# The durations of matmuls that a list scheduler assumes, set to their measured spacing

## The chip, the core and the metric

The kernel runs on one core of a Trainium2 chip. The core has TensorE (PE: matrix products, accumulated in PSUM), VectorE (DVE), ScalarE (ACT), GpSimd (POOL) and SyncE (SP, which here starts loads), each with its own queue of instructions that it takes in order. The metric is the device time of one launch in microseconds (us), the median of several runs.

## What is computed

A forward pass over 512 tokens of width 1024 through three blocks, in float32. The first (layer A) has four gated linear-attention heads of width 192, the second (layer B) twelve banded attention heads of width 64; both add four heads over 256 memory tokens and are followed by a feed-forward part with a short convolution. The third (block 2) has four differential heads, eight heads with a forget gate, and a feed-forward part. Its attention, cut to what matters here:

```python
dq, dk, dv, fq, fk, fv, fg = jnp.split(rmsnorm_2(x, norm1_g) @ w_in, SPLITS, axis=-1)
log_f = jax.nn.log_sigmoid((fg + b_f).astype(f32))
cum = jnp.cumsum(log_f, axis=1)
# four differential heads: two softmaxes, their difference times the values, then a norm
p = softmax(mask(q1 @ k1.T * scale)) - lam * softmax(mask(q2 @ k2.T * scale))
od = rmsnorm_2(p @ dv, subln_g) * (1.0 - lam_init)
# eight gated heads: the scores get the difference of the summed gates
pf = softmax(causal(fq @ fk.T * scale + cum_q - cum_k))
of = pf @ fv
x = x + concat(od, of) @ w_out
x = x + (silu(h2 @ w_gate) * (h2 @ w_up)) @ w_down
```

## The kernel before

Every float32 product is made of three matmuls: each operand is split into a rounded high piece and a low remainder, and high times high, high times low and low times high are summed in one PSUM tile (`mm3`, L420 to L422; in token-major form L440 to L442). Weights come in pieces of 1024 columns by SP into `wr` (2 buffers); `round` (L380) makes the high piece `wh`, on ScalarE or VectorE, and `sub` (L368) the remainder `wl`, on VectorE or GpSimd. Activations `xs` are held as such pairs, feature-major, so that one projection tile `bd` is 8 weight pieces by 3 matmuls of 512 columns.

An attention head goes: keys and queries are split (`kq`; L1126 and L1130 bring the gated heads' keys and queries out of PSUM, L548 and L549 are DMAs on GpSimd's queue that put the pieces in place); scores on TensorE (L556, L558, L559 into `bs`); mask, maximum, exponential and sum (L571, L574, L575, or L568 for the memory heads); a scaling by the reciprocal (L375 on VectorE or GpSimd, or ScalarE); four transposes on TensorE (L586 into `bt`); the split of the probabilities into `pt` (L592 and L593); the product with the values (L605, L606, or L1084 to L1086 for differential heads, into `bo`). A differential head ends with a norm: L1089 clips, a column sum on TensorE (L479), L1094 to L1098 on VectorE, a broadcast of the 512 factors on TensorE (L490), and L1100. In front of the gated heads stands a chain of its own: transposes of the gates (L1103), a copy, a running sum and its split (L1105 to L1116), and for each head the rows that go into the scores (L1135 into `cb`).

The order of every engine's instructions is not the program's. The program is traced once, a list scheduler (class `Order`) walks it with assumed durations (`duration`, L103) and latencies (`LAT`), and the program is traced again with the order found as order-only edges; all waits stay those of the data. At each step a free engine takes the first instruction, in program order, whose operands are ready by the assumed times and whose tiles are to be had: 3 PSUM banks for `bd`, 2 for scores, 2 for `bt`, 1 for `bo`, and so on. So a projection matmul of a later head fills TensorE while an earlier head's softmax is under way, and how many fill it before the softmax is taken to be ready depends on the assumed duration of a matmul against those of the other engines. `other` (L272) gives an idle engine a rounding, remainder or scaling that would wait longer in another's queue; which engine such an instruction runs on is thus set by the same numbers.

## Time and profile before

| | us |
|---|---|
| runs (3): median, lowest, highest | 1939.57, 1938.87, 1941.28 |
| the profiled execution: span | 1938.4 |
| TensorE busy (8628 instructions) | 1861.8, 96% |
| VectorE busy | 1183.9, 61% |
| ScalarE busy | 868.6, 45% |
| GpSimd busy | 323.8, 17% |

The median of the runs is 1.2 us above the span of the profiled execution. The page gives each engine's busy time, a picture of the span in 40 slices, the queues, the chain that ended last and the costliest lines. On TensorE the end of a matmul is modelled, and one in a row shows as 0.39 us where the next starts 0.23 us after it; the spacing of starts is what counts there. By stage: layer A's attention and projections lie in 25 to 290 us, layer B's in 660 to 866, block 2's in 1275 to 1512; the feed-forward parts are 292 to 660, 866 to 1275 and 1512 to 1922.

### The profile page before, as it was taken

How to read it: one execution, taken by the hardware profiler on the slowest of the kernel's cores; microseconds unless marked ns; L12 is line 12 of the kernel's file. 1: busy time of each engine (PE TensorE's matmuls, PEld its weight loads, DVE VectorE, ACT ScalarE, POOL GpSimd, SP SyncE). 2: the span in 40 equal slices, each digit the busy share in tenths (PEclk: the TensorE clock that was granted, in tenths of full speed). 3: DMA queues.
4: the chain of work that ended last, by engine and by line, in shares of the span. 5: the costliest groups of instructions: out<-in, count | busy, mean ns of one | idle time of the engine just before them, and what ended most of it. 6: DMA issues, size and time to landing. Idle time of an engine off the chain costs nothing.

```text
span 1938.4 us, 23991 instructions
## 1 busy us (share of the span) xinstructions
PE 1861.8 (96%) x8628; PEld 1528.4 (79%) x8628; DVE 1183.9 (61%) x2233; ACT 868.6 (45%) x1651; POOL 323.8 (17%) x335
## 2 busy tenths in 40 slices
PE   7999899999999999889999999989998999999997
PEld 7887688888888878768888888878776788888885
DVE  6969776544555667696654455576989754434433
ACT  5567654432444555574442344344657533323332
POOL 2212111100111202131110011141433111001110
PEclk9999899999999999999999999999999999999998
DMA  4223232222223423223222322333321322232222
GB/s 183 92 99 98 82 98 98 98 86 99 98 91 112 160 92 112 87 86 127 88 98 90 106 96 87 97 115 110 93 82 39 120 88 98 93 102 94 94 92 81
DMA packets 59095, 191.93 MB, mean 99 GB/s; under 512 B 7776, under 2 KB 14304, under 8 KB 57184
## 3 DMA queue, kind: packets, MB, share of 16 engines
q1 hardware_dynamic: 54432, 177.81, 27.4%
q0 software_dynamic: 4544, 12.59, 2.5%
q8 instruction: 68, 1.11, 0.2%
q14 instruction: 51, 0.42, 0.1%
HBM read 174.64 MB, written 6.29 MB: 93 GB/s over the span
## 4 chain that ended last, share of the span: by engine, by line
PE 78%; DVE 10%; ACT 2%; issue 1%; DMA 0%; POOL 0%; DVEq 0%; ACTq 0%; POOLq 0%
PE bd L420 23%; PE bd L421 23%; PE bd L422 23%; DVE ae L571 1%; DVE pt L593 1%; DVE ae L375 1%; PE bt L586 1%; PE bd L441 1%; PE bd L440 1%; PE bd L442 1%; DVE wl L368 1%; PE bs L556 1%; DVE kq L368 1%; ACT ae L574 1%; PE bo L605 1%
## 5 line engine op out<-in xcount | busy, mean ns | idle before, releaser
L380 ACT CAST wh<-wr 128x512 fp32r<-128x512 f32 (+2 forms) x574 | 341.6, 596 | 797.1 <-PE bd L421 676.4
L420 PE MATMUL bd<-xs,wh 128*128 128x512 f32 (+1 forms) x1680 | 656.0, 391 | 9.1 <-ACT wh L380 8.0
L422 PE MATMUL bd<-xs,wl 128*128 128x512 f32 (+1 forms) x1680 | 655.3, 390 | 0.0
L421 PE MATMUL bd<-xs,wh 128*128 128x512 f32 (+1 forms) x1680 | 655.0, 390 | 0.0
L368 DVE TENSOR_TENSOR wl<-wr,wh 128x512 fp32r<-128x512 f32 (+2 forms) x590 | 397.8, 676 | 341.7 <-ACT wh L380 332.0
L420 PEld LDWEIGHTS bd<-xs,wh 128*128 128x128 f32 x1680 | 316.7, 189 | 74.4 <-ACT wh L380 8.0
L421 PEld LDWEIGHTS bd<-xs,wh 128*128 128x128 f32 x1680 | 317.0, 189 | 63.7 <-issue 1.9
L422 PEld LDWEIGHTS bd<-xs,wl 128*128 128x128 f32 x1680 | 316.9, 189 | 63.6 <-issue 1.2
L732 POOL TENSOR_TENSOR te<-te,R 128x512 f32<-128x512 f32 x66 | 85.8, 1300 | 830.6 <-ACT te L731 830.6
L422 PE MATMUL bd<-kq,wl 128*128 128x512 f32 x528 | 208.0, 394 | 0.0
L420 PE MATMUL bd<-kq,wh 128*128 128x512 f32 x528 | 208.0, 394 | 0.0
L421 PE MATMUL bd<-pt,wh 128*128 128x512 f32 x528 | 208.0, 394 | 0.0
L422 PEld LDWEIGHTS bd<-kq,wl 128*128 128x128 f32 x528 | 98.7, 187 | 24.5
L421 PEld LDWEIGHTS bd<-pt,wh 128*128 128x128 f32 x528 | 98.7, 187 | 24.4
L420 PEld LDWEIGHTS bd<-kq,wh 128*128 128x128 f32 x528 | 98.7, 187 | 24.4
L735 DVE TENSOR_TENSOR te<-bd,te 128x512 f32<-128x512 f32 x66 | 45.6, 691 | 104.5 <-PE bd L422 98.6
L720 DVE TENSOR_TENSOR te<-bd,R 128x512 f32<-128x512 f32 x66 | 45.6, 691 | 94.5 <-PE bd L422 94.5
L502 POOL TENSOR_TENSOR ae<-ae,ae 128x512 f32<-128x512 f32 x40 | 58.2, 1455 | 246.8 <-ACT ae L498 211.5
L368 POOL TENSOR_TENSOR wl<-wr,wh 128x512 fp32r<-128x512 f32 (+2 forms) x42 | 56.8, 1353 | 177.1 <-ACT wh L380 119.9
L380 ACT CAST kq<-te 128x512 fp32r<-128x512 f32 (+1 forms) x109 | 67.6, 620 | 38.2 <-DVE te L735 32.0
L586 PE MATMUL bt<-ident,ae 128*128 128x128 f32 x304 | 56.4, 286 | 22.8 <-DVE ae L375 9.7
L440 PE MATMUL bd<-wh,xs 128*128 128x384 f32 (+3 forms) x200 | 65.7, 334 | 6.0 <-ACT wh L380 3.0
(260 smaller groups left out, 2237.1 us busy)
## 6 DMA issues: line engine op xcount, KB each, us to landing
wr<-in_w_g SPq DMA_DIRECT2D x66, 512.0 KB, 3.3
wr<-in_w_u SPq DMA_DIRECT2D x66, 512.0 KB, 3.2
wr<-in_w_d SPq DMA_DIRECT2D x48, 512.0 KB, 3.4
wr<-in_w_d SPq DMA_DIRECT2D x48, 192.0 KB, 2.3
kq<-kq POOLq DMA_DIRECT2D x64, 128.0 KB, 3.1
wr<-in_w_qk SPq DMA_DIRECT2D x12, 512.0 KB, 3.2
v<-in_xT SPq DMA_DIRECT2D x4, 1024.0 KB, 8.7
wr<-in_w_o SPq DMA_DIRECT2D x8, 512.0 KB, 3.3
```

The lines of the kernel that those rows point to most:

```text
L368: self.either("DVE", ("DVE", "Pool"), lambda e: e.tensor_tensor(out=out, in0=a, in1=b, op=ALU.subtract))
L375: return e.tensor_scalar(out=out, in0=a, scalar1=s, scalar2=1.0, op0=ALU.mult, op1=ALU.mult)
L380: self.either("Activation", ("DVE", "Activation"), lambda e: (e.copy if e is self.nc.scalar else e.tensor_copy)(out, a))
L420: mm(o, lhsT=wh, rhs=xh, start=start, stop=False)
L421: mm(o, lhsT=wh, rhs=xl, start=False, stop=False)
L422: mm(o, lhsT=wl, rhs=xh, start=False, stop=stop)
L440: mm(pss[b][:, :ncol], lhsT=x[k][0][:, tb], rhs=hi, start=st, stop=False)
L502: (nc.gpsimd if k < 6 else nc.vector).tensor_tensor(out=sq, in0=acc, in1=sq, op=ALU.add)
L586: self.nc.tensor.transpose(o[:, k * 128:(k + 1) * 128], p[:, k * 128:(k + 1) * 128], self.ident)
L720: nc.vector.tensor_tensor(out=g, in0=pg, in1=R, op=ALU.mult)
L732: nc.gpsimd.tensor_tensor(out=s, in0=s, in1=R, op=ALU.mult)
L735: nc.vector.tensor_tensor(out=h, in0=pu, in1=s, op=ALU.mult)
```

## The change

In `duration`, the two numbers for a matmul on TensorE become larger: for float32 pieces (n columns) from n x 0.4167 + 2.6 ns, at least 107, to n x 0.4167 + 13.3, at least 109; for a plain float32 matmul at least 224 instead of 214. The rest of the diff takes comments and docstrings away.

```diff
         if e == "PE":
             if rd[0][7] == F32R:
-                return max(n * 0.4167 + 2.6, 107)
-            return 109 if getattr(ins, "is_transpose", False) else max(4 * n * 0.4167, 214)
+                return max(n * 0.4167 + 13.3, 109)
+            return 109 if getattr(ins, "is_transpose", False) else max(4 * n * 0.4167, 224)
```

The multiset of TensorE's instructions stays. The orders agree in the feed-forward parts and differ in the attention stretches and the start; about 180 roundings, remainders and scalings of those that may run on several engines change engine.

In the rows below, a name with a number is one tile, before the arrow what is written, behind it what is read. On TensorE, at the end of block 2's fourth differential head: `bt_12366` is its column sum, `bt_12382` the gate transposes, `bd_12891` and `bd_12940` are projections of gated heads (keys and queries of the third pair). Before:

```order
L1086 MATMUL bo_12349<-pt_12256,v_10989 128x128
L420 MATMUL bd_12940<-xs_10923,wh_12959 128x512
L421 MATMUL bd_12940<-xs_10924,wh_12959 128x512
L422 MATMUL bd_12940<-xs_10923,wl_12960 128x512
L420 MATMUL bd_12940<-xs_10927,wh_12959 128x512
L421 MATMUL bd_12940<-xs_10928,wh_12959 128x512
L422 MATMUL bd_12940<-xs_10927,wl_12960 128x512
L420 MATMUL bd_12940<-xs_10931,wh_12959 128x512
L421 MATMUL bd_12940<-xs_10932,wh_12959 128x512
L479 MATMUL bt_12366<-cst,oa_12363 128x2 x4
L1103 MATMUL bt_12382<-ident,gates 8x128 x4
L422 MATMUL bd_12940<-xs_10931,wl_12960 128x512
```

And now:

```order
L1086 MATMUL bo_12349<-pt_12256,v_10989 128x128
L422 MATMUL bd_12891<-xs_10927,wl_12911 128x512
L420 MATMUL bd_12891<-xs_10931,wh_12910 128x512
L421 MATMUL bd_12891<-xs_10932,wh_12910 128x512
L422 MATMUL bd_12891<-xs_10931,wl_12911 128x512
L420 MATMUL bd_12940<-xs_10903,wh_12943 128x512
L421 MATMUL bd_12940<-xs_10904,wh_12943 128x512
L422 MATMUL bd_12940<-xs_10903,wl_12944 128x512
L420 MATMUL bd_12940<-xs_10907,wh_12943 128x512
L421 MATMUL bd_12940<-xs_10908,wh_12943 128x512
L479 MATMUL bt_12366<-cst,oa_12363 128x2 x4
L1103 MATMUL bt_12382<-ident,gates 8x128 x4
```

Projections that stood ahead of the column sum and the gate transposes stand behind them: there it was the end of `bd_12940`, here it is its beginning.

On VectorE, from L1089 of that head (`th_12362`) to the start of the gate chain (L1105). `wl_13186`, `wl_13202` and the like are weight remainders, `te_12926` a gated head's keys, `kq_12929` a remainder of them. Before:

```order
L1089 TENSOR_SCALAR th_12362<-bo_12349 128x512
L1094 COPY sm_12371<-bt_12366 128x4
L1097 TENSOR_SCALAR sm_12371<-sm_12371 128x4
L368 TENSOR_TENSOR wl_13202<-wr_13183,wh_13201 128x512
L1130 SCALAR_TENSOR_TENSOR te_12975<-bd_12940,R_10974 128x512
L1096 RECIPROCAL sm_12371<-sm_12371 128x4
L1098 TENSOR_TENSOR sm_12371<-sm_12371 128x4
L486 TENSOR_TENSOR oa_12377<-ident,sm_12371 128x512
L1105 COPY oa_12387<-bt_12382 8x512
```

And now:

```order
L1089 TENSOR_SCALAR th_12362<-bo_12349 128x512
L1126 TENSOR_TENSOR te_12926<-bd_12891,R_10974 128x512
L368 TENSOR_TENSOR wl_13153<-wr_13134,wh_13152 128x512
L368 TENSOR_TENSOR kq_12929<-te_12926,kq_12928 64x512
L1094 COPY sm_12371<-bt_12366 128x4
L1097 TENSOR_SCALAR sm_12371<-sm_12371 128x4
L380 CAST wh_13185<-wr_13183 128x512
L1096 RECIPROCAL sm_12371<-sm_12371 128x4
L368 TENSOR_TENSOR wl_13186<-wr_13183,wh_13185 128x512
L1098 TENSOR_TENSOR sm_12371<-sm_12371 128x4
L486 TENSOR_TENSOR oa_12377<-ident,sm_12371 128x512
L1105 COPY oa_12387<-bt_12382 8x512
```

L1126, the remainders `wl_13153`, `kq_12929` and `wl_13186` and a rounding have come in between L1089 and L1105; `wl_13202` and L1130 have left.

On GpSimd, during the first gated heads: `kq` are halves of keys and queries, `ae` probabilities. Before:

```order
L548 DMA kq_13170<-kq_13170 64x512
L368 TENSOR_TENSOR kq_13171<-te_13168,kq_13170 64x512
L549 DMA kq_13171<-kq_13171 64x512
L548 DMA kq_13172<-kq_13172 64x512
L368 TENSOR_TENSOR kq_13173<-te_13168,kq_13172 64x512
L549 DMA kq_13173<-kq_13173 64x512
L375 TENSOR_SCALAR ae_12992<-ae_12992,sm_12987 128x128
L375 TENSOR_SCALAR ae_13019<-ae_13019,sm_12987 128x384
L368 TENSOR_TENSOR kq_13219<-te_13217,kq_13219 64x512
L368 TENSOR_TENSOR kq_13220<-te_13217,kq_13220 64x512
```

And now:

```order
L368 TENSOR_TENSOR kq_13171<-te_13168,kq_13170 64x512
L548 DMA kq_13170<-kq_13170 64x512
L549 DMA kq_13171<-kq_13171 64x512
L548 DMA kq_13172<-kq_13172 64x512
L375 TENSOR_SCALAR ae_12867<-ae_12867,sm_12820 128x512
L549 DMA kq_13173<-kq_13173 64x512
L368 TENSOR_TENSOR wl_13458<-wr_13442,wh_13457 128x384
L375 TENSOR_SCALAR ae_13019<-ae_13019,sm_12987 128x384
L375 TENSOR_SCALAR ae_13067<-ae_13067,sm_13062 128x128
L368 TENSOR_TENSOR kq_13220<-te_13217,kq_13220 64x512
```

Of the remainders `kq_13171`, `kq_13173`, `kq_13219` and `kq_13220` two have gone to VectorE, and the DMA of `kq_13170` (keys of the fourth pair) stands behind one.

## Rows read from the trace of the kernel before

**Rows 1.** Busy time of each engine, with share of the span and instructions (page).

```profile
PE 1861.8 (96%) x8628; PEld 1528.4 (79%) x8628; DVE 1183.9 (61%) x2233; ACT 868.6 (45%) x1651; POOL 323.8 (17%) x335
```

**Rows 2.** TensorE timeline in a feed-forward stretch: start, duration, engine, line, operation.

```profile
900.51 0.39 PE L420 MATMUL bd<-xs,wh 128*128 128x512 f32 x1
...
907.33 0.39 PE L420 MATMUL bd<-xs,wh 128*128 128x512 f32 x1
```

**Rows 3.** Busy time by window: stretch, its length, then each engine.

```profile
core 0: us, PE busy (x) PEld busy (x) DVE busy (x) ACT busy (x) POOL busy (x), PEclk, DMA share, GB/s
190.00:230.00 40.00, 36.81 (x173) 27.31 (x172) 30.19 (x76) 25.31 (x62) 8.06 (x12) 0.94 0.30 99
800.00:866.00 66.00, 56.02 (x277) 45.64 (x276) 52.18 (x151) 42.85 (x107) 18.41 (x28) 0.93 0.31 88
1350.00:1420.00 70.00, 66.53 (x316) 50.27 (x314) 67.71 (x179) 44.14 (x97) 32.72 (x39) 1.00 0.31 94
1460.00:1512.00 52.00, 42.35 (x242) 32.27 (x241) 49.38 (x169) 41.45 (x113) 17.21 (x21) 1.00 0.12 31
1680.00:1800.00 120.00, 120.00 (x523) 97.71 (x523) 45.80 (x71) 34.13 (x56) 6.46 (x5) 1.00 0.29 98
```

**Rows 4.** TensorE's waits, whole span: us in total, times, longest.

```profile
PE bt L586 <- DVE ae L375: 9.7, 16, 1.3
```

**Rows 5.** TensorE timeline around the gate chain, in brackets idle before and releaser.

```profile
1449.80 0.95 PE L479 MATMUL bt<-cst,oa 128*128 128x2 f32 x8
1450.61 0.60 PE L1103 MATMUL bt<-ident,gates 128*8 128x128 f32 x4
...
1460.19 0.39 PE L422 MATMUL bd<-xs,wl 128*128 128x512 f32 x1
1461.84 0.33 PE L558 MATMUL bs<-cb,cb 128*128 128x128 f32 x1 [1.26 <-DVE cb L1135]
...
1469.03 0.48 PE L422 MATMUL bd<-xs,wl 128*128 128x512 f32 x1
```

**Rows 6.** VectorE timeline in the same stretch.

```profile
1445.24 0.69 DVE L593 TENSOR_TENSOR pt<-bt,pt 128x512 fp32r<-128x512 f32 x1 [0.83 <-ACT pt L592]
...
1448.10 0.69 DVE L1089 TENSOR_SCALAR th<-bo 128x512 f32<-128x512 f32 x1 [1.43 <-PE bo L1086]
1450.79 0.16 DVE L1094 COPY sm<-bt 128x4 f32<-128x4 f32 x1 [2.00 <-PE bt L479]
...
1451.55 0.69 DVE L368 TENSOR_TENSOR wl<-wr,wh 128x512 fp32r<-128x512 f32 x1 [0.40 <-PE bd L422]
1452.16 0.68 DVE L1130 SCALAR_TENSOR_TENSOR te<-bd,R 128x512 f32<-128x512 f32 x1
...
1457.21 0.42 DVE L1112 CAST cb<-oa 8x512 fp32r<-8x512 f32 x1
1457.55 0.41 DVE L1114 TENSOR_SCALAR oa<-oa 8x512 f32<-8x512 f32 x1
...
1461.30 0.88 DVE L1135 TENSOR_SCALAR cb<-cb,cst 128x512 fp32r<-128x512 f32 x2
```

**Rows 7.** VectorE timeline: a remainder beside GpSimd's, and one alone.

```profile
1438.96 1.58 DVE L368 TENSOR_TENSOR kq<-te,kq 64x512 fp32r<-64x512 f32 x1
...
1440.76 0.69 DVE L368 TENSOR_TENSOR kq<-te,kq 64x512 fp32r<-64x512 f32 x1
```

**Rows 8.** GpSimd timeline at that time.

```profile
1438.61 1.39 POOL L368 TENSOR_TENSOR wl<-wr,wh 128x512 fp32r<-128x512 f32 x1
```

**Rows 9.** TensorE timeline, layer A, end of the memory attention.

```profile
225.01 0.39 PE L556 MATMUL bs<-kq,kq 128*128 128x256 f32 x1 [0.66 <-ACT ae L574]
225.24 0.28 PE L559 MATMUL bs<-kq,kq 128*128 128x256 f32 x1
225.47 1.98 PE L490 MATMUL bo<-oa,cst 128*128 128x512 f32 x2
...
229.06 0.80 PE L605 MATMUL bo<-pt,kq 128*128 128x512 f32 x1 [1.18 <-DVE xs L932]
```

**Rows 10.** Window at the lower granted clock (column PEclk).

```profile
225.60:235.80 10.20, 8.23 (x20) 4.77 (x20) 6.08 (x16) 4.12 (x13) 0.00 (x0) 0.50 0.00 0
```


## The prediction

> **What bounds the kernel now.** First the busy times [rows 1]: TensorE works 1861.8 us of a span of 1938.4, so all its waits together are 76.6 us, and no order of instructions can win more than that, apart from what the clock costs. Then the windows by stage [rows 3]. In a feed-forward stretch (1680 to 1800 us) TensorE is busy 120.00 of 120.00 us: nothing to win there, however its rows are dealt. The waits lie in the attention stretches: 3.19 us in 190 to 230, 9.98 in 800 to 866, 3.47 in 1350 to 1420, 9.65 in 1460 to 1512. In those VectorE is the near rival: 67.71 of 70 us in 1350 to 1420, 49.38 of 52 in 1460 to 1512. Third, the list of TensorE's waits [rows 4]: the largest entry is 16 waits of the softmax transposes (L586) on VectorE's scaled probabilities, 9.7 us in all and 1.3 at most. So no single wait rules; there are many short ones, each on a chain of softmax steps between TensorE, ScalarE and VectorE.
>
> The spacing of matmuls tells what the edited numbers are. Between 900.51 and 907.33 us [rows 2] lie 30 starts of 512-column matmuls: 6.82 / 30 = 0.2273 us each. The table before assumes 512 x 0.4167 + 2.6 = 215.9 ns, the new one 226.6.
>
> **What the change moves.** It issues no other instructions: the same matmuls, in another order, and some roundings, remainders and scalings on another engine. So TensorE's 1861.8 us stay, and only waits can change. In the feed-forward stretches the two orders agree row by row. In the attention stretches the planner now takes TensorE for 5% slower, so in its plan a softmax step is ready after fewer projection matmuls, and attention rows move ahead of them.
>
> *Block 2, 1350 to 1512 us.* The place that decides is the end of the fourth differential head and the gate chain, which the first forget-gated head needs. Before, the column sum (L479) starts at 1449.80 and the gate transposes (L1103) at 1450.61, then projections run to 1460.19, and the first gated score (L558) starts at 1461.84 after a wait of 1.26 us for VectorE's L1135 [rows 5]. On VectorE [rows 6] this looks so: it idles 0.83 before 1445.24, 1.43 before 1448.10 (for L1086), 2.00 before 1450.79 (for L479) and 0.40 before 1451.55, in all 4.66 us, while TensorE works through projections; then it is packed to L1135 at 1461.30. In the new order 18 projection matmuls of 512 columns fewer stand ahead of L479 and L1103: 18 x 0.2273 = 4.1 us earlier. That is less than the 4.66 us that VectorE idles there, so VectorE could begin all 4.1 us sooner.
>
> It doesn't keep all of it. Between L1089 and L1135 the new list of VectorE gains one L1126, two wl remainders, one kq remainder and one rounding, and loses one wl and one L1126: two 512-column rows net, at 0.61 us (the start at 1452.16 less that at 1451.55) and a cast at 0.34 (1457.55 less 1457.21) [rows 6]: +1.56 us. This is worth 4.1 - 1.56 = 2.5 us at the first gated score. The waits of TensorE from there to 1512 are on VectorE, which has 49.38 busy of 52 us [rows 3].
>
> Behind L1135, three kq remainders that GpSimd did are VectorE's now: 3 x 0.61 = +1.8 us. (On GpSimd's queue one DMA of the fourth pair's keys moves behind a remainder; six gated heads are scored before it is needed, which hide it.) Against that stand four fewer remainders on GpSimd from the end of the fourth head to 1512. What one of those costs VectorE shows at 1438.61: while GpSimd's remainder runs for 1.39 us [rows 8], VectorE's own, which takes 0.69 at 1440.76, takes 1.58 at 1438.96 [rows 7]: 0.89 more. Not every one hits: I take half, 0.45, with bounds of 0 and 0.89. Four times 0.45 is 1.8, so the two cancel; the bounds are +1.8 and -1.8 us. The Trainium skill, SBUF — State Buffer, section "Who interferes with whom", says that a VectorE instruction with two SBUF inputs and a GpSimd instruction that reads SBUF exclude each other for a whole instruction; the trace agrees as far as these rows go (0.69 against 1.58 us). By that rule a remainder moved to VectorE would be nearly free wherever GpSimd's had blocked it (0.61 paid, up to 0.89 returned), and the sum would be lower by 1.8 us.
>
> Where the hidden part is uncovered: bringing attention forward leaves projections for later. Before, the last of them starts at 1469.03 [rows 5]; in the new order they are threaded among the gated heads for some 90 rows more. They can fill TensorE's waits there (9.65 us in 1460 to 1512), so I cost them at nothing; if each delays the row behind it on the chain, the price is a matmul, 0.23 us, a few times.
>
> *Layer A, memory attention, 190 to 230 us.* Scores and transposes come 1 to 11 rows earlier, from the same point on the rows agree again. One row goes the wrong way: the broadcast (L490) at 225.47 stands behind one more pair of scores. On it hang VectorE's L931 and L932, and TensorE's wait of 1.18 us at 229.06 [rows 9]. A pair costs 0.46 us (225.47 less 225.01). Against it, the earlier scores and transposes can win no more than that wait of 1.18 us, since the rows around it then start on time. Bounds +0.5 and -1.2; no row tells which end is nearer, and I take the middle, -0.4.
>
> *Layer B, 745 to 866, and the start.* The first scores of each half come two rows earlier, but they wait for keys that other engines make: two rows are 2 x 0.227 = 0.45 us that TensorE would wait instead of work, twice, unless the rows behind make it up. VectorE's work there is even between the orders to about 1 us. Price 0, bounds -1.5 and +1.5.
>
> **The sum.** -2.5 (block 2, first gated score) + 0 (rest of the gated heads) - 0.4 (layer A) + 0 (layer B) = -2.9 us on the profiled execution, 1938.4 to 1935.5. The median of the runs, 1939.57, is 1.2 us above that span; the same distance gives 1936.7 us.
>
> The clock. From 225.6 to 235.8 the granted clock is 0.50, the 1.2 GHz level [rows 10], right behind TensorE's waits in layer A; four shorter stretches are like it. Whether they stay depends on where waits fall. In that window TensorE is busy 8.23 us, so the level costs up to 4.1 us; gaining or losing such a stretch is in the range, not in the sum.
>
> **The rivals.**
> (a) *More than forecast.* VectorE's two added rows and the cast fit into its 4.66 us of idle time, so that all 4.1 us arrive; four fewer blocked remainders return 0.89 each, 3.6, against 1.8; layer A gives 1.2. Sum -4.1 - 1.8 - 1.2 = -7.1: 1932.5. For it: the idle time on VectorE is real, and on TensorE's side. Against: 4.66 less 4.1 leaves 0.56 for 1.56 of work.
> (b) *Nothing.* VectorE is busy 67.71 of 70 us in 1350 to 1420 [rows 3]; its own list, not TensorE's, then sets when L1089 of the fourth head comes, and with the same list of work the earlier TensorE rows only wait earlier. Sum 0: 1939.6, between 1938 and 1941.
> (c) *Slower.* VectorE is the bound from 1455 us on, gains nothing from an earlier L1103, and carries the 1.56 and the 1.8 us without a return from GpSimd; layer A's L490 costs 0.46 and layer B's early scores 2 x 0.45. Sum +4.7: 1944.3. It decides as soon as VectorE's idle time ahead of L1094 (2.00 us) is no longer there to be filled. For it: 49.38 of 52 us busy. Against: the 4.66 us are there in the trace of before.
> (d) *The old numbers are the true ones.* If a 512-column matmul took 215.9 ns, the new table would plan TensorE too slow: the 18 rows moved would make it wait up to 4.1 us, 1943.7. Rows show 227.3 ns, so I give it 2 in 100. The Trainium skill, TensorE: Matmul & The Clock Gate, section "Back-to-back issue gap", has N / 2.4 GHz plus about 2.5 ns, 215.8 ns at 512 columns, which is the old table; for these float32 pieces the trace does not agree with it.
>
> **How the numbers follow.** Forecast (1934.5 to 1939) 0.38; (a) 0.24; (b) 0.22; (c) 0.14; (d) 0.02. What a measurement of this kernel can tell from no change is about 0.2%, 3.9 us: faster is under 1935.7, slower over 1943.4. All of (a) and 0.14 of the forecast's 0.38 are faster: 0.38. The rest of the forecast and (b), with a hundredth of (c), are the same: 0.47. The rest of (c), and (d): 0.15. For the range: (a) with half a stretch at half clock gone besides (2 us) is 1930.5; (c) is 1944.3. So 1930.5 to 1944.5.
>
> **What would show it.** In the new profile: L1103 about 4 us ahead of its old time relative to the projections, VectorE's waits for L1086 and L479 of 1.43 and 2.00 us shrunk to under 1 together, the first L558 near 1459.3, and the waits in 1460 to 1512 no larger than 9.65 us; the feed-forward stretches unchanged at full busy time; in layer A L490 some half a microsecond later than the transposes around it. I am wrong if the first L558 starts no earlier (then (b) or (c) by the later waits), if the gain at L558 is there and gone by the output projection (the three remainders, or projections in the way of the gated heads), or if stretches at clock 0.50 appear or vanish.

## The result, and the profile after

The changed kernel takes 1951.91 us (median of 4 runs, 1948.35 to 1954.32), the kernel before in the same session 1939.22 (4 runs, 1938.35 to 1941.28). The ratio is 1.0060, 95% interval 1.0045 to 1.0074: slower by about 12 us, where 3 us less were forecast, and outside the range. The profiled execution has a span of 1950.1 us, 11.7 more than before.

The first row of the page answers to [rows 1]:

```profile
PE 1868.9 (96%) x8628; PEld 1527.5 (78%) x8628; DVE 1186.0 (61%) x2237; ACT 863.2 (44%) x1647; POOL 316.0 (16%) x335
```

TensorE is busy 7.1 us longer with the same 8628 instructions, so not even its busy time stayed. Its waits grew from 76.6 to 81.2 us. The list of its waits (us in total, times, longest) has changed its head:

```profile
PE bd L420 <- ACT wh L380: 8.4, 1, 8.4
PE bt L490 <- DVE oa L486: 7.2, 7, 4.2
PE bt L586 <- DVE pt L593: 6.4, 11, 1.1
PE bt L479 <- DVE ae L502: 5.1, 2, 2.8
PE bt L586 <- DVE sm L575: 4.1, 6, 1.2
PE bd L441 <- DVE wl L368: 3.7, 2, 2.6
PE bd L440 <- ACT wh L380: 3.6, 1, 3.6
```

The softmax transposes' 9.7 us behind L375 [rows 4] are gone from the head of the list, as the earlier attention rows were to do (3.1 us are left there; all waits of L586 together fall from 21.8 to 18.1). In their place two entries have grown on which the prediction has no word: the column sums (L479) behind VectorE's sums of squares (L502), from 2.5 to 5.1 us, and a token-major projection (L441) behind a weight remainder (L368), from 1.6 to 3.7, of which 2.6 at once.

To see where the 11.7 us came in, I follow the same matmul in both traces and take how much later it starts; this is called its drift. It is 0.0 at 24 us, +3.5 at 36, +4.8 at 60, +6.7 at 230, +10.1 at 748, +6.1 at 870, +7.0 at 1285, +12.4 at 1300, +10.8 at 1345, +9.7 at 1480 and +10.9 at 1900. Two jumps stand out, in the first 36 us and at 1285 to 1300, neither in a stretch that the sum had priced above zero. A drift compares two executions, and these differ by themselves: the run below with the new numbers in layer B alone has before's order on every engine up to 290 us, and its drift there is -3.0, 2.3 of it from 160 us on, where the stretch at clock 0.50 of [rows 10] is absent. So the drift tells where time goes in one execution, and the medians of the runs tell what a change costs. Two windows at those places and one in layer B, of before and then of after (columns as in [rows 3]):

```profile
24.00:60.00 36.00, 34.09 (x181) 30.01 (x182) 27.87 (x54) 20.28 (x37) 5.23 (x6) 1.00 0.29 96
750.00:870.00 120.00, 101.53 (x526) 83.44 (x525) 98.82 (x292) 80.04 (x202) 36.71 (x56) 0.94 0.31 86
1285.00:1320.00 35.00, 30.89 (x162) 28.87 (x163) 20.79 (x34) 11.27 (x23) 14.33 (x11) 0.95 0.40 132
```

```profile
24.00:60.00 36.00, 32.05 (x162) 28.13 (x161) 24.67 (x48) 17.37 (x33) 6.74 (x8) 0.92 0.30 96
750.00:870.00 120.00, 102.62 (x547) 82.19 (x547) 98.62 (x290) 79.91 (x206) 36.67 (x62) 1.00 0.33 91
1285.00:1320.00 35.00, 27.48 (x129) 24.11 (x129) 26.84 (x33) 12.08 (x21) 21.78 (x15) 0.85 0.35 118
```

In the first window TensorE issues 162 matmuls instead of 181, in the third 129 instead of 162, at a lower granted clock. In layer B it is the other way: two stretches of 6.8 us at clock 0.50 that the trace of before has there are gone (0.94 to 1.00), and about 4 us come back. The order is not shown to be the reason: with the new numbers in layer B alone, where TensorE's list in layer B is that of after, two such stretches stand there again, at 793.8 and 841.6 us.

*The start.* VectorE of before: two roundings beside GpSimd's work, and one alone (start, duration):

```profile
21.82 1.89 DVE L380 CAST wh<-wr 128x392 fp32r<-128x392 f32 x1
...
28.76 1.45 DVE L380 CAST wh<-wr 128x392 fp32r<-128x392 f32 x1
...
32.29 0.35 DVE L380 CAST wh<-wr 128x392 fp32r<-128x392 f32 x1
```

VectorE of after, and below it the matmul that waits:

```profile
25.38 2.56 DVE L380 CAST wh<-wr 128x392 fp32r<-128x392 f32 x2
27.86 1.75 DVE L456 SCALAR_TENSOR_TENSOR xs<-v,vec,xs 128x512 fp32r<-128x512 f32 x1
29.54 0.55 DVE L368 TENSOR_TENSOR wl<-wr,wh 128x392 fp32r<-128x392 f32 x1
...
30.14 0.53 PE L441 MATMUL bd<-wl,xs 128*128 128x392 f32 x1 [2.59 <-DVE wl L368]
```

GpSimd of after at that time:

```profile
25.31 1.03 POOL L368 TENSOR_TENSOR wl<-wr,wh 128x392 fp32r<-128x392 f32 x1
26.31 2.75 POOL L502 TENSOR_TENSOR ae<-ae,ae 128x512 f32<-128x512 f32 x2
```

The planner has moved one rounding (tile wh_349, wh81 in an expectation below) from ScalarE to VectorE, and another of VectorE's (wh_383) has come forward behind it. The two now take 2.56 us, against 0.35 for the one alone, while GpSimd's remainder and sums of squares run beside them; the remainder that TensorE needs (wl_350) stands behind them, and TensorE waits 2.59 us.

*The norms between block 1 and block 2.* VectorE, TensorE and GpSimd of before, then of after:

```profile
1287.53 1.48 DVE L502 TENSOR_TENSOR ae<-ae,ae 128x512 f32<-128x512 f32 x2
...
1292.27 0.95 PE L479 MATMUL bt<-cst,ae 128*128 128x2 f32 x8
...
1289.15 11.07 POOL L1190 TENSOR_TENSOR v<-v,th 128x512 f32<-128x512 f32 x8 [3.69 <-ACT th L1177]
```

```profile
1296.08 0.36 DVE L380 CAST wh<-wr 128x384 fp32r<-128x384 f32 x1 [2.42 <-PE bo L442]
1298.05 3.43 DVE L502 TENSOR_TENSOR ae<-ae,ae 128x512 f32<-128x512 f32 x2
...
1301.63 1.02 PE L479 MATMUL bt<-cst,ae 128*128 128x2 f32 x8 [2.77 <-DVE ae L502]
...
1296.42 7.75 POOL L1190 TENSOR_TENSOR v<-v,th 128x512 f32<-128x512 f32 x5 [4.06 <-ACT th L1177]
```

VectorE's list of rows is the same in both orders from 1280 to 1300 us of before. Before, its two sums end at 1289.0, just ahead of GpSimd's products (L1190). After, VectorE first waits 2.42 us for a weight buffer, because TensorE's last matmul on that buffer (L442) now stands behind the broadcast L490; so the two sums fall beside the products and take 3.43 us instead of 1.48, and TensorE waits 2.77 us where it waited for nothing.

*Where the prediction looked.* The rows of after that answer to [rows 5] and [rows 9]:

```profile
232.09 2.05 PE L490 MATMUL bo<-oa,cst 128*128 128x512 f32 x2
...
235.75 0.79 PE L605 MATMUL bo<-pt,kq 128*128 128x512 f32 x1 [1.61 <-DVE xs L932]
...
1457.30 1.05 PE L479 MATMUL bt<-cst,oa 128*128 128x2 f32 x8
1458.21 0.60 PE L1103 MATMUL bt<-ident,gates 128*8 128x128 f32 x4
...
1470.75 0.47 PE L558 MATMUL bs<-cb,cb 128*128 128x128 f32 x1 [2.00 <-DVE cb L1135]
```

And the windows that answer to rows of [rows 3] and [rows 10], shifted by the drift:

```profile
231.70:241.90 10.20, 8.01 (x19) 4.51 (x20) 5.35 (x14) 3.64 (x11) 0.00 (x0) 0.50 0.06 23
...
1471.00:1523.00 52.00, 46.72 (x260) 37.80 (x260) 48.33 (x169) 41.43 (x115) 15.84 (x21) 0.94 0.12 31
1691.00:1811.00 120.00, 120.00 (x524) 97.72 (x523) 45.67 (x70) 34.10 (x56) 6.47 (x5) 1.00 0.31 98
```

The feed-forward stretch is as full as before. In block 2, L479 and L1103 are later by 7.5 and 7.6 us, less than the drift of 10.8 with which the stage begins: 3.3 and 3.2 us are won there. The waits in the gated heads fell from 9.65 to 52 - 46.72 = 5.28 us (a part of that is a stretch of 3.4 us at clock 0.50, which lengthens busy time by up to 1.7).

### The profile page after: what moved, and what is told of

Same layout as the page of the kernel before. It is cut to its first block, busy times and chain, and to the rows that moved or that the text cites. A ratio compares the mean times of both kernels' runs of the same rounds, so it can differ in the third digit from the quotient of the medians.

```text
span 1950.1 us, 24017 instructions
## 1 busy us (share of the span) xinstructions
PE 1868.9 (96%) x8628; PEld 1527.5 (78%) x8628; DVE 1186.0 (61%) x2237; ACT 863.2 (44%) x1647; POOL 316.0 (16%) x335
## 4 chain that ended last, share of the span: by engine, by line
PE 80%; DVE 13%; ACT 3%; issue 2%; DMA 2%; POOL 0%; DVEq 0%; ACTq 0%; POOLq 0%; SPq 0%
PE bd L421 23%; PE bd L420 23%; PE bd L422 22%; DVE wl L368 2%; PE bd L441 1%; PE bd L442 1%; PE bd L440 1%; PE bt L586 1%; DVE kq L368 1%; DVE pt L593 1%; DVE ae L571 1%; DVE wh L380 1%; DVE te L821 1%; PE bs L556 1%; PE bo L606 1%
## 5 line engine op out<-in xcount | busy, mean ns | idle before, releaser
L380 ACT CAST wh<-wr 128x512 fp32r<-128x512 f32 (+1 forms) x574 | 341.7, 596 | 796.3 <-PE bd L421 659.2
L368 DVE TENSOR_TENSOR wl<-wr,wh 128x512 fp32r<-128x512 f32 (+2 forms) x596 | 402.6, 678 | 357.8 <-ACT wh L380 347.0
L502 POOL TENSOR_TENSOR ae<-ae,ae 128x512 f32<-128x512 f32 x40 | 57.3, 1432 | 255.5 <-ACT ae L498 197.7
L380 ACT CAST kq<-te 128x512 fp32r<-128x512 f32 (+1 forms) x109 | 67.7, 621 | 40.0 <-DVE te L735 30.6
L586 PE MATMUL bt<-ident,ae 128*128 128x128 f32 x304 | 56.0, 288 | 18.7 <-DVE pt L593 6.4
L368 POOL TENSOR_TENSOR wl<-wr,wh 128x512 fp32r<-128x512 f32 (+3 forms) x36 | 45.6, 1268 | 173.1 <-ACT wh L380 107.4
L441 PE MATMUL bd<-wl,xs 128*128 128x384 f32 (+3 forms) x200 | 67.1, 336 | 3.7 <-DVE wl L368 3.7
```

The lines of the kernel that those rows point to most:

```text
L368: self.either("DVE", ("DVE", "Pool"), lambda e: e.tensor_tensor(out=out, in0=a, in1=b, op=ALU.subtract))
L380: self.either("Activation", ("DVE", "Activation"), lambda e: (e.copy if e is self.nc.scalar else e.tensor_copy)(out, a))
L441: mm(pss[b][:, :ncol], lhsT=x[k][0][:, tb], rhs=l, start=False, stop=False)
L502: (nc.gpsimd if k < 6 else nc.vector).tensor_tensor(out=sq, in0=acc, in1=sq, op=ALU.add)
L586: self.nc.tensor.transpose(o[:, k * 128:(k + 1) * 128], p[:, k * 128:(k + 1) * 128], self.ident)
```

## The experiments

All were timed in five rounds against the kernel before; every ratio is to it, with its 95% interval.

### The new numbers in one stage alone

The table gives the new numbers only where the tile that a TensorE instruction writes has a number in a range; elsewhere the old ones stand.

```diff
-                return max(n * 0.4167 + 13.3, 109)
+                return max(n * 0.4167 + 13.3, 109) if self.new(outs) else max(n * 0.4167 + 2.6, 107)
+    def new(outs):
+        i = int(outs[0][0].split("_")[-1])
+        return 0 <= i < 700      # the start; 700-2700 layer A; 5350-7860 layer B;
+                                 # 10870-11300 norms; 11300-13700 block 2's attention
```

> The new numbers hold only for the first stage (setup, layer A's norm and first value projection, to about 70 us); the rest is planned with the old ones, and its order is that of before but for some engine choices in layer A. Theory A (the loss sits in a few moved rows, and the stage differences between the two profiles add up): +4.8 us, of which 3.1 by 45 us (a remainder on VectorE that now stands behind two roundings which GpSimd holds up) and 1.8 from a half-clock stretch at 57 to 61 us. Rival B (any other order meets the clock gate at other points; the stage does not matter): anywhere from -3 to +7, not tied to rows before 45 us. Rival C (the difference is all in attention, as the prediction had it, and the start is worth nothing): 0 +- 1.

> The new numbers for layer A alone (heads and memory attention, 70 to 290 us). Theory A: the two profiles drift apart by 1.9 us there, so about +2. The prediction's price for layer A was -0.4, with bounds of -1.2 and +0.5. Rival B: any value from -3 to +4.

> The new numbers hold only for layer B (keys and values, band and memory attention, output projection; 660 to 866 us). Theory A: the profiles differ by +2.9 us up to 760 and by -4.5 from there to 866, with both 6.8 us stretches at half clock gone: -1.6 us in all, and the two stretches stay away. Rival B: the stretches were a matter of phase, they are here again at 0.50, and the sum is 0 to +3. Prediction's own price: 0 +- 1.5.

> The new numbers hold only for the two norms and the value projections in front of block 2's attention (1270 to 1340 us). VectorE's list is that of before but for one row. Theory A: +4.4 us as between the two profiles; VectorE's L380 waits about 2.4 us for the value projection's L442 of the bank bo, and the sum of squares (L502 on VectorE) runs beside GpSimd's L1190 at 3.4 us instead of 1.5. Rival B (clock phase): 0 to +2, with no such wait. Rival C (engine choices and GpSimd's contention make the loss): 0, since none changes here.

> The new numbers for block 2's attention alone (1340 to 1512 us). The prediction: -2.5 us, from column sum and gate transposes that come 18 projection matmuls earlier. Theory A, from the two profiles: they drift apart by 2.2 us to 1450, win 3.3 back to 1480 (the 18 rows are real there) and lose 0.9 behind it, with two half-clock stretches of 3.4 us that before did not have: 0 +- 1 in all. If the stretches are away in the profile of this run, -1 to -3.

| new numbers in | time, us | ratio | 95% interval | drift won or lost in the stage |
|---|---|---|---|---|
| the start | 1943.87 | 1.0020 | 1.0009 to 1.0031 | +3.4 by 36 us, +4.9 by 60 |
| layer A | 1944.55 | 1.0025 | 1.0015 to 1.0036 | +2.1 by 100, +3.7 by 400 |
| layer B | 1938.89 | 1.0000 | 0.9991 to 1.0009 | none that lasts |
| norms | 1944.18 | 1.0018 | 1.0010 to 1.0027 | +4.6 by 1300, +3.8 by 1315 |
| block 2's attention | 1938.83 | 0.9997 | 0.9988 to 1.0006 | -2.5 by 1480, -1.6 at its end |

The five add up to +0.60%, the whole loss. As each of the five is known to about 0.1% only, and places do not simply add (next run), so close a match is partly chance. The profiled execution of the kernel with new numbers at the start is the fastest of its eleven (1938.97 us): it wins the 4.9 us back by 870 us, in stages that have before's order. The 0.20% is from the median of the eleven. Three stages lose, and block 2, which bore nearly all of the predicted gain, wins no more than a measurement can tell. The rows of block 2 alone, TensorE's and VectorE's:

```profile
1444.71 1.05 PE L479 MATMUL bt<-cst,oa 128*128 128x2 f32 x8
1445.62 0.60 PE L1103 MATMUL bt<-ident,gates 128*8 128x128 f32 x4
...
1458.17 0.33 PE L558 MATMUL bs<-cb,cb 128*128 128x128 f32 x1 [2.02 <-DVE cb L1135]
...
1457.64 0.88 DVE L1135 TENSOR_SCALAR cb<-cb,cst 128x512 fp32r<-128x512 f32 x2
```

The stage begins 1.74 us early in this execution. L479 is 5.09 us earlier than in [rows 5], so 3.35 are due to the new order (4.1 predicted); the first gated score is 3.67 earlier, so 1.9 (2.5 predicted).

New numbers everywhere but at the start and the norms:

> The new numbers everywhere but for the start (to about 70 us) and block 2's norms (1270 to 1340 us), which are planned with the old ones. Theory A (the loss is made at places, and they add up): new at the start alone measured +4.0 us and new at the norms alone +4.3, so this should stand 8.3 below the changed kernel, at +4.2 us over before. Rival B (the loss belongs to no place; a changed order costs a few us wherever it is): still +8 or more over before. Rival E (the two places are the whole loss): 0 +- 1 over before.

Measured: 1948.17 us, 1.0042 (1.0030 to 1.0054), 8 us where 4 were expected: rival B's number (8 or more). The places do not simply add. Layer A's loss, which after does not show beside the start's delay, comes out when the start is mended (drift +2.1 between 60 and 100 us, against none in after). But layer A is in the stages taken alone too, and those planned anew here add up to 0.22%, half of what was measured. The other half has no cause shown; in the profiled execution 2.1 us of it come in from 650 to 870 us, and 1.7 at the norms, which have the old numbers here.

### The start: one rounding

The new numbers at the start, and the planner may not give the rounding of wh_349 to another engine:

```diff
-                if k in self.flex and e in self.flex[k][1] and wait + ...
+                if k in self.flex and self.acc[k][0][0][0].split("_")[-1] not in ("349",) and e in ...
```

> As the run with the new numbers at the start alone, but one rounding (the weight piece whose remainder TensorE waits for, wh81) may not move from ScalarE to VectorE. The remainder wl82 then stands behind one rounding and one activation piece on VectorE instead of behind two roundings and a piece. Theory A (the remainder is late because VectorE's roundings ahead of it are held up by GpSimd's sums): TensorE's wait for it shrinks from 2.6 us to about 1, and the drift at 36 us from +3.2 to +1.5 or less. Rival F (the earlier column sum on TensorE makes the loss): drift unchanged at +3.2.

Measured: 1941.68 us, 1.0008 (0.9999 to 1.0018). The drift at 36 us goes from +3.21 to -0.19; as this execution begins 0.8 us early, 0.6 us of the stage's 3.4 are left. The waiting matmul, with the rounding on VectorE, and with it back on ScalarE, below it VectorE's two roundings of this run:

```profile
29.89 0.44 PE L441 MATMUL bd<-wl,xs 128*128 128x392 f32 x1 [2.59 <-DVE wl L368]
```

```profile
26.93 0.45 PE L441 MATMUL bd<-wl,xs 128*128 128x392 f32 x1 [0.22 <-DVE wl L368]
...
24.55 0.35 DVE L380 CAST wh<-wr 128x392 fp32r<-128x392 f32 x1
...
28.49 1.45 DVE L380 CAST wh<-wr 128x392 fp32r<-128x392 f32 x1
```

TensorE's list is the same in both runs, so its moved rows (rival F) are not the cause. VectorE has no fewer roundings for this edit: the planner gave it wh_367 from ScalarE instead, which takes 0.35 us at 24.55, and wh_383, 1.45 us beside a sum on GpSimd, now stands behind the remainder that TensorE waits for. So the start's 3 us are the two roundings that stood ahead of that remainder while GpSimd worked, 2.56 us together, and not the number of roundings on VectorE.

### The norms: three rows

The old numbers, with TensorE's list changed by hand behind the planner: first only L490 (tile 10891) put one row earlier, then also L479 (10958) and L490 (10972) four rows earlier each, as the new numbers have them (the diff is the second run's).

```diff
+    def swap(self, e, ks):
+        for tile, d in (("10891", 1), ("10958", 4), ("10972", 4)) if e == "PE" else ():
+            p = [p for p, k in enumerate(ks) if self.acc[k][0][0][0].split("_")[-1] == tile]
+            m = [ks.pop(p[0]) for _ in p]
+            ks[p[0] - d:p[0] - d] = m
+        return ks
```

> The order of before with two neighbours on TensorE exchanged: the norm's broadcast (L490 into bt) now stands ahead of the value projection's last matmul of one weight piece (L442 into bo). Nothing else differs on any engine. Theory A: this one row is the whole of the loss at the norms: +4.4 us (at least +3), since the weight buffer that this matmul reads is given back 4 us later, VectorE's next rounding waits for it, and behind that stands the sum of squares, which then collides with GpSimd. Rival D (the other rows moved at the norms, 16 or so, carry part of it): +1 to +3. Rival B: 0 +- 1.

Measured: 1941.12 us, 1.0005 (0.9996 to 1.0013). The chain is there (VectorE waits 2.41 us, the sums take 3.45, L479 waits 1.17), but the drift grows by 1.7 us only.

> The order of before with three rows of TensorE at block 2's norms placed as the new numbers place them: the first broadcast (L490) one row earlier, the second column sum (L479) and the second broadcast (L490) four rows earlier each. All other engines as before. Theory A in its corrected form (one row alone cost 1.7 by 1315 us in its profile, and an early reduction row that waits on VectorE holds up the matmuls behind it): drift at 1315 us of +3 to +4, as with all of the new numbers there (+3.9), and a time of +2 to +4. Rival: the rest of the rows (the order of value projections from 1306 us) carries it: drift +1.7 as with the one row.

Measured: 1943.51 us, 1.0020 (1.0011 to 1.0029), the loss of the norms as a whole. VectorE and TensorE:

```profile
1288.67 0.36 DVE L380 CAST wh<-wr 128x384 fp32r<-128x384 f32 x1 [2.04 <-PE bo L442]
1290.62 3.44 DVE L502 TENSOR_TENSOR ae<-ae,ae 128x512 f32<-128x512 f32 x2
...
1294.21 1.84 PE L479 MATMUL bt<-cst,ae 128*128 128x2 f32 x8 [2.41 <-DVE ae L502]
```

Part of it is the clock: behind this wait the granted clock is 0.50 for 6.8 us from 1293.9, where before has none, so up to 3.4 us are its price. The run of the norms alone has the same 6.8 us at 1293.8, after has them at 1303.5, and the run with one row moved, where L479 waits 1.17 us, has 3.4 us at 1293.8. That the clock falls is tied to the wait only by this place; no run separates the two.

### Layer A: two roundings

In layer A TensorE's list is the same in both orders up to 117 us, yet 2.1 us are lost by 100. There GpSimd has taken two remainders from VectorE (wl_888, wl_926; wl185 and wl192 in the expectation), and VectorE two roundings from ScalarE (wh_887, wh_925), while one (wh_909) went the other way. The edit of the start is used again, first with the tiles 888 and 926, then with 887 and 950.

> As the run with the new numbers for layer A alone, but two weight remainders (wl185, wl192) may not move from VectorE to GpSimd. TensorE's order stays that of the run with the new numbers. Theory G (layer A's loss by 100 us, TensorE's wait of 1.5 us for L860, comes of three remainders on GpSimd where before had one, each of which holds VectorE up by 0.8): the wait at about 100 us is gone or under 0.4, and the drift by 100 us falls from +2.1 to +0.5 or less; the time falls by 1 to 2 us against that run. Rival H (the moved rows of TensorE make it): wait and drift as in that run.

Measured: 1944.73 us, 1.0024 (1.0015 to 1.0033); TensorE still waits for L860:

```profile
100.05 0.44 PE L440 MATMUL bd<-wh,xs 128*128 128x384 f32 x1 [1.44 <-DVE th L860]
```

So the wait does not need GpSimd's two remainders. This alone does not clear them, since the planner also dealt the roundings anew: wh_925 went back to ScalarE and wh_950 came to VectorE, which again has two of ScalarE's roundings ahead of L860. The drift from 60 to 100 us falls from 2.1 to 1.3.

> The kernel with the new numbers in layer A alone lost 0.25%, 1.4 us of it at about 100 us where TensorE's L440 waits 1.47 us for VectorE's L860. Here two roundings that this order had moved to VectorE (the tiles wh_887 and wh_925) go back to ScalarE, and with them two remainders to VectorE; TensorE's rows stay. Theory A (the roundings stand ahead of L860 in VectorE's row and delay it): the wait at 100 us falls to under 0.7 us and the drift by 230 us from about +2.7 to about +1.5 or less; ratio 1.001 to 1.0015. Rival B (it is the order of VectorE's other rows, L825 before L816): the wait stays at 1.3 to 1.5 us, ratio 1.0025.

The matmul that waits, with the new numbers in layer A, and then with the two roundings back on ScalarE:

```profile
100.55 0.44 PE L440 MATMUL bd<-wh,xs 128*128 128x384 f32 x1 [1.47 <-DVE th L860]
```

```profile
100.62 0.44 PE L440 MATMUL bd<-wh,xs 128*128 128x384 f32 x1 [0.50 <-DVE th L860]
```

Measured: 1943.99 us, 1.0021 (1.0013 to 1.0030). In the order that this edit gives, wh_887, wh_925 and wh_950 are on ScalarE and both remainders on VectorE. From the run before it differs in two rows alone, wh_887 and wh_950, which are ScalarE's here and VectorE's there; TensorE's wait falls from 1.44 to 0.50 us with them. From 60 to 100 us the drift now grows by 0.34 us instead of 2.08. So the roundings ahead of L860 are the cause of that step. The ratio is above the 1.001 to 1.0015 expected: the rest of layer A's loss, 100 to 400 us, is still there (2.4 us of drift), and what makes it stays open. (This execution's drift has 1.6 us more from a half-clock stretch at 55.5 us.)

### Is it the number, or any new order?

Other values in the same two lines; for the fourth kernel the new numbers with the other engines' durations at their measured means.

```diff
-                return max(n * 0.4167 + 13.3, 109)                 # 226.6 ns at 512 columns
+                return max(n * 0.4167 + 8, 109)                    # 221.3, step_of_a_third
+                return max(n * 0.4167 + 24, 109)                   # 237.3, beyond_the_measured
+                return max(n * 0.4167 - 9.3, 101)                  # 204.0, shorter_than_the_old
-            return 69 + (0.52 if fast and not psum else 1.04) * n + 61 * (scalars > 0)
+            return 69 + 1.0 * n if op == "TensorCopy" and not psum else 1.16 * (69 + ...)
-            return (53 if psum else 93) + 0.8333 * n + ...
+            return 1.2 * ((53 if psum else 93) + 0.8333 * n + ...)
-            return 150 + 2.1 * n
+            return 1.18 * (150 + 2.1 * n)                          # these three: all_numbers_measured
```

> The assumed time of a 512-column matmul is 221.3 ns here, halfway between the old 215.9 and the new 226.6; the float32 row gets 219. If the loss follows the number (an order is worse the longer TensorE is taken to be), the ratio is about 1.003. If each number just deals another order, whose luck has nothing to do with the number's truth, the ratio can fall anywhere from 0.998 to 1.007, with the places of loss not those of the new table: at the start no rounding of wh_81 on VectorE (its list there is nearly the old one), so no 3.2 us at 36 us; by the old table's row order at the norms no 2.77 us wait.

> The assumed time of a 512-column matmul is 237.3 ns here, 10.7 more than the new table's 226.6 and 10 more than the measured 227.3. If an order gets better as the number nears the spacing measured (and the loss came from elsewhere), this one is worse than the new table: over 1.006. If the loss grows with the number: 1.009 to 1.012. If each number is another draw: anywhere from 0.998 to 1.010, and no trend over the three numbers.

> The assumed time of a 512-column matmul is 204.0 ns here, 11.9 under the old 215.9, and the float32 row 202; all other engines as before, so the ratio of a remainder to a matmul is 2.95. Theory R: no slower than before, 0.995 to 1.001. Rival T: 1.004 to 1.010, as on the other side of the old number (+5.4 ns gave 1.0054, +10.7 gave 1.006, +21.4 gave 1.0116).

> The new numbers for TensorE, and for the other engines their measured means in the kernel before in place of the planner's undisturbed ones: VectorE's casts 69 + 1.0 n (584 ns measured at 512 columns, 335 assumed), its other work x1.16 (699 against 601), ScalarE x1.2 (622 against 520), GpSimd x1.18 (1442 against 1225). Theory R (what the plan needs is the ratio of TensorE's number to the others'; the old table had 601/216 = 2.78 for a remainder over a matmul, the new one 2.65, the chip has 699/227 = 3.08): the loss is gone, ratio 0.995 to 1.001. Rival T (the kernel before is a lucky or searched order, and every other table deals a worse one): 1.004 to 1.010.

| a 512-column matmul taken as | time, us | ratio | 95% interval | drift at 290, 1285, 1315, 1900 us |
|---|---|---|---|---|
| 204.0 ns | 1947.11 | 1.0036 | 1.0024 to 1.0048 | -2.9, -0.6, +0.5, +6.9 |
| 215.9 (before) | 1939.87 | 1 | | |
| 221.3 | 1951.15 | 1.0054 | 1.0042 to 1.0067 | +4.5, +8.9, +12.5, +14.8 |
| 226.6 (after) | 1951.91 | 1.0060 | 1.0045 to 1.0074 | +6.7, +7.0, +10.8, +10.9 |
| 237.3 | 1961.99 | 1.0116 | 1.0101 to 1.0131 | +17.3, +16.0, +20.0, +21.9 |
| 226.6, all engines measured | 1940.77 | 1.0008 | 0.9999 to 1.0016 | -3.9, -2.4, -0.5, +2.4 |

Upward the loss does not shrink (221.3 and 226.6 cannot be told apart, 237.3 costs twice as much). Correcting the other engines too takes it away, as theory R forecast; but the shorter number, which by R should have cost nothing, costs 0.36%, close to rival T's range. So R as stated falls, and T falls by the kernel with all numbers measured. At 221.3 ns the start has no loss (drift -0.04 at 36 us), as expected, but the norms lose 5 us again by 1300 (3.6 by 1315), which was not: there too the broadcast L490 stands ahead of L442, and L479 waits 1.88 us for the sums. What stands is: with the other engines' numbers left as they are, 215.9 ns gives the best of five orders, and its being further from the 227.3 ns of the chip [rows 2] doesn't hurt. The kernel with all numbers measured has gains and losses of several us too (-5.7 us of drift from 160 to 290, +3.1 from 1315 to 1515). Whether there is a rule behind these orders or each is a new draw, six tables cannot settle.

### Taking the collision away

In the two places that were cleared up most, VectorE meets GpSimd's sums of squares or is late with its own. The sums can all be VectorE's:

```diff
-                (nc.gpsimd if k < 6 else nc.vector).tensor_tensor(out=sq, in0=acc, in1=sq, op=ALU.add)
+                nc.vector.tensor_tensor(out=sq, in0=acc, in1=sq, op=ALU.add)
```

> The old numbers, but all sums of squares of the norms (L502) on VectorE; before has five of seven on GpSimd. A try for a faster kernel. Theory G (GpSimd's tensor operations hold up VectorE's with two SBUF inputs and its casts by 0.8 to 1.5 us each, at the start and at block 2's norms): VectorE's queue is shorter although it has more to do, the waits of TensorE at 1283 to 1287 us (4.1) and at 23 to 32 us (2.7) shrink by 2 to 4 us together, -2 to -5 us in all. Rival (VectorE is the bound there and five sums of 0.6 us each cost 3 us more): +1 to +3.

With the old numbers: 1934.55 us, 0.9968 (0.9957 to 0.9978), faster than both kernels. The groups of L502 (busy, mean ns) before, and then with all sums on VectorE:

```profile
L502 DVE TENSOR_TENSOR ae<-ae,ae 128x512 f32<-128x512 f32 x16 | 11.0, 687 | 2.5 <-ACT ae L498 2.3
...
L502 POOL TENSOR_TENSOR ae<-ae,ae 128x512 f32<-128x512 f32 x40 | 58.2, 1455 | 246.8 <-ACT ae L498 211.5 <-issue 19.2 <-DVE v L1179 14.9
```

```profile
L502 DVE TENSOR_TENSOR ae<-ae,ae 128x512 f32<-128x512 f32 x56 | 43.6, 779 | 3.3 <-ACT ae L498 1.9
```

The busy times of that kernel, from its page:

```profile
PE 1861.5 (96%) x8628; PEld 1529.0 (79%) x8628; DVE 1180.5 (61%) x2259; ACT 872.5 (45%) x1660; POOL 274.3 (14%) x300
```

VectorE takes on 40 sums and is busy 3.4 us less than before. Only a part of this is the collision: matched instruction by instruction, the 40 sums take 30.8 us, but the planner also moves 19 roundings, remainders and scalings off VectorE (21.8 us in the trace of before) and five on to it (2.3 us), and the 2094 instructions that VectorE has in both kernels take 12.8 us less. The drift is -2.5 at 36 us, and a further -4.0 comes at the norms. At the start the collision is seen to be gone: the casts of 128x392 take 0.36 us at 22.60 and 0.35 at 28.70, where before had 1.89 and 1.45, and TensorE's waits of 1.26 and 1.41 us for VectorE's L380 and L368 have no counterpart. How much of the whole gain is the planner's other moves no run separates.

> As the run before, with the new numbers everywhere. If the loss of the changed kernel comes of rows and remainders that run into GpSimd's sums at the start and at the norms (4.0 and 4.3 us), most of it goes with the sums: 2 us or less above the run with the old numbers. If the new order is worse by itself, the gap stays at 8 to 12 us.

With the new numbers: 1941.42 us, 1.0007 (0.9997 to 1.0018). The gap between new and old numbers falls from 12 to 7 us, not to the 2 that the first theory wanted and less than the 8 of the other. Against the run before, which has the same sums and the old numbers, the norms lose 1.6 us from 1285 to 1315 where they lost 3.7. But the start still loses 2.8 us by 40 (3.1 without the sums moved): the wait of 2.59 us is gone, and others have come, 1.51 us for L486 at 37.31 among them. So the new order loses there without this collision too, and in layer A it loses 1.9 us more (60 to 290 us).

> All sums of squares on VectorE, the new numbers for block 2's attention alone, the old ones elsewhere. Sums on VectorE alone gave 0.9968; the new numbers in block 2's attention alone gave 0.9997, a gain of 1.7 us in the trace. If the two are independent, 0.9960 to 0.9966 (1931.5 to 1933). Rival: the sums leave VectorE's idle time in block 2 as it was, but the other planner state deals block 2 anew, and the gain is lost: 0.9970 to 0.9985.

With the new numbers in block 2's attention alone: 1933.53 us, 0.9965 (0.9953 to 0.9977). It cannot be told from the sums alone, so that neither the independent gain nor its loss is shown, and it too beats both kernels.

## Why the prediction was wrong

The sum put two terms at a gain and two at nothing; the gains came out at about nothing, and the loss lies in a term put at nothing and in places that had no term.

1. *Block 2, first gated score, -2.5 us.* The mechanism was right, its size a little too large: 1.9 us at the first gated score, 2.5 by 1480, 1.6 at the end of the stage. The 18 rows brought L479 forward by 3.35 us and not 4.1; VectorE's added rows took 1.4 of that back (1.56 in the sum), and TensorE's wait for L1135 rose from 1.26 to 2.02 us. In the time of the kernel it can't be told from nothing.
2. *"Layer B, and the start": price 0, bounds of 1.5 us either way.* This is the step that failed first. For layer B zero holds (1.0000). The start alone costs 0.20%, 4.0 us between the medians. I had compared TensorE's rows there and VectorE's work in sum, and not asked which engine each rounding had moved to. That a rounding's price depends on what runs beside it could be read before: VectorE's casts at 21.82 and 28.76 us take 1.89 and 1.45 us in the trace of before, the one at 32.29 us 0.35.
3. *Layer A, memory attention, -0.4 us.* I priced 40 us of layer A and took the rest as even. In those 40 us TensorE's wait at L605 did not shrink but rose from 1.18 to 1.61 us, and with the new numbers in layer A alone the drift does not change there (2.7 at 190 and at 230 us). The loss starts by 100 us, where TensorE's list is the same and only the lists of VectorE, ScalarE and GpSimd differ: 0.25% in all.
4. *The norms, 1270 to 1310 us,* have no term at all. Three short pieces of TensorE's list have moved there by one to four rows (a few projection matmuls have changed places besides), and VectorE's list up to the sums is the same; I took so small a difference for nothing. Moved by hand, the three rows cost 0.20%.
5. *"TensorE's 1861.8 us stay, and only waits can change"* is wrong: busy time rose by 7.1 us. Outside the end of the span, stretches at clock 0.50 add up to 30.6 us before and 37.4 after; 6.8 us more cost up to 3.4 of the 7.1, and the rest stays open. The range allowed for one such stretch to come or go, the sum for none.

Rival (c) had the sign right and the place wrong: VectorE did not become the bound from 1455 us on. Rival (b)'s number fits block 2 taken alone (0.9997), its mechanism does not: L479 came 3.35 us earlier. Rival (d) fails in its mechanism: the spacing is 227.3 ns [rows 2], and the 18 rows that it had waiting for up to 4.1 us brought the first gated score forward by 1.9. That the old number all the same gives the best of five orders is not explained by any run.

## What to carry to other kernels

- When a list scheduler's table is edited, compare the lists of all engines at every stage, above all which engine took a flexible instruction, and price a moved instruction at what it takes beside its new neighbours (0.35 or 1.45 us), not by itself.
- Three short rows that moved by one to four places cost more (0.20%) than eighteen moved together could win (nothing that the time shows): look for the last use of a buffer that another engine waits for, and for a pair of operations on VectorE and GpSimd that had just missed each other.
- One number made true in a table of numbers that are all too short need not make the plan better (1.0060; with all engines' numbers true 1.0008). Here taking work from the engine that collides (the sums on GpSimd) won more, 0.32%, than any of the tables tried.

## What was not expected of the hardware

- How much a collision costs an operation as short as a cast: two casts of 128x392 took 2.56 us beside a remainder and sums on GpSimd, one alone 0.35; two sums of squares took 3.43 us beside GpSimd's products, 1.48 without. The Trainium skill, SBUF — State Buffer, section "Who interferes with whom", says that copies and casts on VectorE can enter a mode in which they take the pair of ports that GpSimd uses, and that whoever issues first blocks the other for a whole instruction. The casts agree with it (0.35 against 2.56 us for two); the sums are operations with two inputs, as the remainders are, for which alone I had weighed that section.
- Moving 40 additions from GpSimd (58.2 us there) to VectorE left VectorE's busy time no larger (1183.9 to 1180.5 us), because the planner moved 19 other rows off it and the rows that stayed took 12.8 us less.
- Stretches at granted clock 0.50 fall elsewhere in other executions, and not only where the order differs. After has them at 30.4 and 57.7 us, where before has none, and none at 795 and 850 us. But the one from 225.6 us in before (10.2 us) is there with the three rows moved (225.5), stands as two of 3.4 us with the new numbers in block 2's attention (224.4 and 231.2), and is absent with them in layer B, while the order up to there is the same in all four.
